# Gate products of a product-key expert layer: the layout of the one-hots and of the numbers and gates they are made from

## The chip, the cores and the metric

The kernel runs on one core of one Trainium2 chip, as one launch. The metric is the time of that launch on the device in microseconds (us); the median of the runs is what counts. TensorE multiplies matrices into PSUM (the accumulation memory), VectorE, ScalarE and GpSimd do elementwise work, and SyncE issues the DMAs. In the views of the profile these are PE (matmuls), PEld (the weight loads of TensorE), DVE, ACT, POOL and SP.

## The reference, cut to what matters

The reference is a transformer block with an attention, a state space mixer and a layer of product-key experts, then two more blocks. The change touches the experts alone:

```python
def peer_mixer(xn, w_query, sub_keys, u_tab, v_tab):
    ...                                  # t = 256 tokens, d = 1024
    vals, idx = lax.top_k(s, PEER_TOPK)  # per head: 16 best of 128 keys on each side
    ...
    i1 = jnp.take_along_axis(idx[:, :, 0], pos // PEER_TOPK, axis=-1)
    i2 = jnp.take_along_axis(idx[:, :, 1], pos % PEER_TOPK, axis=-1)
    expert = (i1 * N_SUB_KEYS + i2).reshape(t, PEER_HEADS * PEER_TOPK)
    gate = jax.nn.softmax(best, axis=-1).reshape(t, PEER_HEADS * PEER_TOPK)
    ...
        a = jnp.einsum('cd,ced->ce', xb, u_tab[eb]).astype(jnp.float32)
        w = (gb * jax.nn.gelu(a, approximate=False)).astype(xb.dtype)
        return jnp.einsum('ce,ced->cd', w, v_tab[eb])
```

Each token has 8 heads x 16 choices = 128 choices, each with a first number i1 and a second number i2 (0 to 127) and a gate. There are 128 x 128 experts.

## The kernel before, in words

The kernel gathers no rows. It computes the activation of every expert for every token, multiplies it by a gate that is zero for experts that were not chosen, and multiplies the result by the whole second table. The function `peer` holds both passes. The tile `store` has, for each partition (the first number), 128 x 256 values: second number by token.

First pass (`gemm_t(128, 8, xh, xl, evict, step=step)`): 128 steps, one for each second number. Each step takes one 512 KB piece of the first table, which SyncE loads, ScalarE rounds to a high part `whi` (L121, two halves) and VectorE or GpSimd subtracts to a low part `wlo` (L123); three buffers of each exist. TensorE then does 24 matmuls of a 128 x 128 weight with 256 tokens (L206 to L208), `evict` applies the GELU on ScalarE (L979, L982), and, for tokens whose gates are known already, VectorE multiplies by the gate (L980). After each step `step` runs pieces of the background work: first `topk`, which finds the choices in two halves of 128 tokens, chiefly on VectorE, and then the gate products, spread evenly over the steps up to number 126.

`topk` ends each half with three TensorE transposes (L1096) of i1, i2 and the gates into PSUM, with the choice on the partition and the token along the row. L1097 copies both kinds of numbers to the 16-bit tile `ids`, L1098 and L1099 write the gate, times 1024, as a high and a low 16-bit part to `gts`.

A gate product is made by `quad(q)` for four tokens at a time, 64 times. For one token the 128 x 128 gates are the product of two one-hots over the choices: A (choice by first number), which is the weight that TensorE loads, and B (choice by second number, each row times the choice's gate, as a high part Bh and a low part Bl), which TensorE moves through. So a quad has 8 matmuls of 128 x 128 with 128 columns (L964, L965), each with a weight load of its own, into one PSUM tile `g`. VectorE multiplies what the first pass has already stored by it (L969) and ScalarE copies the rest (L971). `onehots(q)` makes the operands on VectorE one quad ahead, in two instructions of 1024 elements on each partition: L951 compares `io4` (the numbers 0 to 127, each four times) with the numbers of four tokens, for A and for the unscaled B at once; L952 multiplies by both gate parts. In these tiles the four tokens are innermost: for one token both A and B are read with a step of four 16-bit elements.

```python
v.tensor_tensor(out=AB, in0=io4.unsqueeze(1).to_broadcast(both), in1=b(ids), op=OP.is_equal)
v.tensor_tensor(out=B, in0=AB[:, 1].unsqueeze(1).to_broadcast(both), in1=b(gts), op=OP.mult)
```

Second pass: 128 steps of `gemm_acc` with the second table (L274 to L276, 512 columns each), whose weights come from `store` (L1009, L1010). It begins when all gates are in `store`. Layers of the other block follow.

The order of instructions on each engine is set by the planner of the tile framework, from the order in the program and from priorities (background work has a later one, `LATE`); engines work through their lists in order and wait for each other by semaphores.

Of the kernel before, what the change touches and what calls it, by code (L numbers as in the profile page):

```python
# [9 lines left out]
F16 = mybir.dt.float16  # L10
U32 = mybir.dt.uint32
AF = mybir.ActivationFunctionType
OP = mybir.AluOpType
# [4 lines left out]
T = 256  # L18
# [50 lines left out]
XR = 4  # L69
# [129 lines left out]
class Kernel:  # L199
# [698 lines left out]
    def peer(self):  # L898
        tc, nc, a = self.tc, self.nc, self.a
        v, g, s, te = nc.vector, nc.gpsimd, nc.scalar, nc.tensor  # L900
        self.bg = Background(tc, LATE)
        with ExitStack() as outer:
            pst = outer.enter_context(tc.tile_pool(name="pstore", bufs=1))
            store = pst.tile([128, 128, T], F32, name="store")
            self.tail_base = 76
            flat = store[:, self.tail_base:].rearrange("p a b -> p (a b)")
            off = [0]

            def scratch(shape, dt=F32):
                n = int(np.prod(shape[1:]))  # L910
                x = flat[:, off[0]:off[0] + n]
                off[0] += n
                if dt != F32:
                    x = x.bitcast(dt)
                if len(shape) == 2:
                    return x
                names = "abcd"[:len(shape) - 1]
                kw = {c: d for c, d in zip(names, shape[1:])}
                return x.rearrange(f"p ({' '.join(names)}) -> p {' '.join(names)}", **kw)

            with ExitStack() as ctx:
                w = ctx.enter_context(tc.tile_pool(name="pu", bufs=1))
                self.acc, tp, gp = self.banks(0, 1, 2), self.banks(7, 6), self.banks(3, 4, 5)
                xh, xl = self.tokens()
                for i in range(2):
                    self.norm_h(i, self.gain, xh, xl, tp)
                iota = scratch([128, 128])
                nc.sync.dma_start(iota, a["iota"])
                sk = scratch([128, 8, 128])
                nc.sync.dma_start(sk, a["subkeys"])  # L930
                io4 = w.tile([128, 128, 4], F16, name="io4")
                v.tensor_copy(io4, iota.unsqueeze(2).to_broadcast([128, 128, 4]))

                qT = scratch([128, 8, T])
                self.gemm_t(8, 8, xh, xl, lambda m, ps: s.copy(qT[:, m], ps))

                ids = w.tile([128, 2, T], F16, name="ids")
                gts = w.tile([128, 2, T], F16, name="gts")
                self.bg.add(self.topk(w, tp, scratch, qT, sk, iota, ids, gts))
                done = {"t": 0, "c": 0, "q": 0, "oh": {}, "from": None}  # L940

                spare = self.const.tile([128, 2, 2, 128, 4], F16, name="spare", tag="gain")
                both = [128, 2, 128, 4]

                def onehots(q):


                    b = lambda x: x[:, :, 4 * q:4 * q + 4].unsqueeze(2).to_broadcast(both)
                    AB = self.stay.tile(both, F16, name="oh", tag="xr", bufs=XR)
                    B = spare[:, q % 2]  # L950
                    v.tensor_tensor(out=AB, in0=io4.unsqueeze(1).to_broadcast(both), in1=b(ids), op=OP.is_equal)  # L951
                    v.tensor_tensor(out=B, in0=AB[:, 1].unsqueeze(1).to_broadcast(both), in1=b(gts), op=OP.mult)  # L952
                    done["oh"][q] = AB[:, 0], B[:, 0], B[:, 1]

                def quad(q):
                    c = done["c"]
                    if q not in done["oh"]:
                        onehots(q)
                    if q + 1 < T // 4:
                        onehots(q + 1)  # L960
                    A, Bh, Bl = done["oh"].pop(q)
                    ps = gp.tile([128, 4, 128], F32, name="g", tag="g")
                    for t in range(4):
                        te.matmul(ps[:, t], A[:, :, t], Bh[:, :, t], start=True, stop=False)  # L964
                        te.matmul(ps[:, t], A[:, :, t], Bl[:, :, t], start=False, stop=True)  # L965
                    p = ps.rearrange("p t i -> p i t")
                    o = store[:, :, 4 * q:4 * q + 4]
                    if c:
                        v.scalar_tensor_tensor(o[:, :c], p[:, :c], 1.0 / 1024, o[:, :c], op0=OP.mult, op1=OP.mult)  # L969
                    if c < 128:  # L970
                        s.activation(o[:, c:], p[:, c:], AF.Copy, scale=1.0 / 1024)  # L971
                    done["t"] = 4 * q + 4
                    done["q"] = q + 1

                def evict(m, ps):
                    t = done["t"]
                    if t:
                        tmp = w.tile([128, T], F32, name="gt", tag="gt", bufs=2)
                        s.activation(tmp[:, :t], ps[:, :t], AF.Gelu)  # L979
                        v.tensor_tensor(out=store[:, m, :t], in0=tmp[:, :t], in1=store[:, m, :t], op=OP.mult)  # L980
                    if t < T:
                        s.activation(store[:, m, t:], ps[:, t:], AF.Gelu)  # L982
                    done["c"] = m + 1

                def step():
                    c = done["c"]
                    self.bg.step(STEP(c))
                    if done["from"] is None:
                        if not self.bg.q:
                            done["from"] = c  # L990
                        return
                    want = (T // 4 * (c - done["from"])) // (LAST - done["from"])
                    while done["q"] < min(want, T // 4):
                        quad(done["q"])

                self.gemm_t(128, 8, xh, xl, evict, step=step)
                while done["q"] < T // 4:
                    quad(done["q"])

            with ExitStack() as ctx:  # L1000
                w = ctx.enter_context(tc.tile_pool(name="pv", bufs=1))
                ps = self.acc4(5, 6, 7, 3)
                self.next_gain("attn_norm_0")
                parts = {}

                def split(c):
                    wh = w.tile([128, T], F32R, name="wh", tag="wh", bufs=3)
                    wl = w.tile([128, T], F32R, name="wl", tag="wl", bufs=3)
                    s.copy(wh, store[:, c])  # L1009
                    v.tensor_tensor(out=wl, in0=store[:, c], in1=wh.bitcast(F32), op=OP.subtract)  # L1010
                    parts[c] = wh, wl

                def lhs(c):
                    if c == 0:
                        split(0)
                        split(1)
                    if c + 2 < 128:
                        split(c + 2)
                    return parts[c]

                self.gemm_acc(range(128), Once(lhs), ps, self.residual)

    def topk(self, w, tp, scratch, qT, sk, iota, ids, gts):
        nc = self.nc
        v, g, s, te = nc.vector, nc.gpsimd, nc.scalar, nc.tensor
# [23 lines left out]
        for i in range(2):  # L1049
            ts = slice(128 * i, 128 * i + 128)  # L1050
            for hg in range(2):
                ps = [tp.tile([128, 4, 128], F32, name="tp", tag="tp") for _ in range(2)]
# [8 lines left out]
            for h in range(8):  # L1061
                for k in range(2):
# [4 lines left out]
                                in0=vals[:, h, 0].unsqueeze(2).to_broadcast([128, 16, 16]),  # L1067
                                in1=vals[:, h, 1].unsqueeze(1).to_broadcast([128, 16, 16]), op=OP.add)
# [3 lines left out]
            p = pos.rearrange("p h k -> p (h k)")  # L1072
# [5 lines left out]
            for k in range(2):  # L1078
                v.tensor_tensor(out=eq, in0=pf[:, k].unsqueeze(1).to_broadcast([128, 16, 16, 8]),
                                in1=io16.unsqueeze(2).to_broadcast([128, 16, 16, 8]), op=OP.is_equal)  # L1080
# [13 lines left out]
            ps = tp.tile([128, 4, 128], F32, name="tp", tag="tp")  # L1094
            for k in range(3):
                te.transpose(ps[:, k], e3[:, k], self.ident)  # L1096
            v.tensor_copy(ids[:, :, ts], ps[:, 0:2])  # L1097
            v.tensor_scalar(gts[:, 0, ts], ps[:, 2], 1024.0, None, op0=OP.mult)  # L1098
            v.scalar_tensor_tensor(gts[:, 1, ts], ps[:, 2], 1024.0, gts[:, 0, ts], op0=OP.mult, op1=OP.subtract)  # L1099
            yield  # L1100


# [569 lines left out]
```

## Time and profile before

| what | us |
|---|---|
| median of 3 runs | 1787.24 (1787.05 to 1788.32) |
| the profiled execution | 1782.35 |
| its span, first to last instruction | 1780.6 |
| PE busy | 1703.5 (96%) |
| PEld busy | 1488.6 (84%) |
| DVE busy | 1086.8 (61%) |
| ACT busy | 869.0 (49%) |
| POOL busy | 638.6 (36%) |

The times of rows come from the profiled execution. In a group of instructions the first number is the busy time, the second the mean of one, and after the bar stands the engine's idle time just before them and what ended it. A matmul's recorded duration is longer than its share of the stream, since matmuls overlap: the distance between starts tells what one costs. The first gate product starts 478.0 us after the start of the span and the last at 765.9 us.

### The profile page before, as it was taken

To read this page: it belongs to the slowest core of one execution; us is meant where nothing else is said; L and a number is where in the kernel's file an instruction comes from. 1 tells how busy PE (TensorE), PEld (TensorE's weight loads), DVE (VectorE), ACT (ScalarE), POOL (GpSimd) and SP (SyncE) were. 2 spreads that over 40 slices of the span, in tenths; PEclk is the share of its full clock that TensorE was granted. 3 is DMA by queue.
4 is the path that set the end of the run, shared out by engine and by line. 5 is a ranking of instruction groups with operands and counts; after the bars stand their busy time and mean duration, and the time that the engine had idled before them with its cause. 6 is when DMAs were issued, how large, how long until landed. Compare 5 with 4: busy or idle time off the path is not lost.

```text
span 1780.6 us, 29967 instructions
## 1 busy us (share of the span) xinstructions
PE 1703.5 (96%) x10732; PEld 1488.6 (84%) x10732; DVE 1086.8 (61%) x2496; ACT 869.0 (49%) x2048; POOL 638.6 (36%) x529
## 2 busy tenths in 40 slices
PE   7989998989899999999999999899999999999998
PEld 4457987988899999988888888787899878779986
DVE  6877443589777778855555555677754246875422
ACT  2113544544454444445555555556565455656643
POOL 1020375677400000034444444331444443145443
PEclk9989999999999999999999999999999999999999
DMA  7322445444544444456665656534456664335554
GB/s 228 109 80 72 142 133 166 154 156 143 156 150 144 143 145 149 146 166 190 195 195 192 196 192 192 177 96 143 150 182 190 189 194 139 119 119 190 189 190 142
DMA packets 81537, 282.33 MB, mean 159 GB/s; under 512 B 9659, under 2 KB 12524, under 8 KB 81388
## 3 DMA queue, kind: packets, MB, share of 16 engines
q1 hardware_dynamic: 81388, 280.41, 49.5%
q8 instruction: 85, 1.39, 0.3%
q14 instruction: 64, 0.52, 0.1%
HBM read 279.30 MB, written 1.07 MB: 157 GB/s over the span
## 4 chain that ended last, share of the span: by engine, by line
PE 77%; DVE 12%; POOL 4%; issue 3%; ACT 2%; DMA 2%; POOLq 0%; SPq 0%; DVEq 0%; ACTq 0%
PE acc L276 10%; PE acc L275 10%; PE acc L274 10%; PE acc L208 10%; PE acc L206 10%; PE acc L207 10%; PE acc L219 2%; POOL wlo L123 2%; PE g L964 2%; PE g L965 2%; PE o L1390 1%; PE acc L242 1%; PE acc L243 1%; PE acc L244 1%; DVE wlo L123 1%
## 5 line engine op out<-in xcount | busy, mean ns | idle before, releaser
L123 POOL TENSOR_TENSOR wlo<-raw,whi 128x512 fp32r<-128x512 f32 (+2 forms) x420 | 554.2, 1333 | 913.2 <-ACT whi L121 884.3
L121 ACT CAST whi<-raw 128x512 fp32r<-128x512 f32 (+2 forms) x940 | 544.7, 613 | 436.6 <-PE acc L207 179.3
L123 DVE TENSOR_TENSOR wlo<-raw,whi 128x512 fp32r<-128x512 f32 (+1 forms) x520 | 407.4, 797 | 326.8 <-ACT whi L121 316.0
L208 PE MATMUL acc<-xh,wlo 128*128 128x256 f32 x1664 | 473.7, 285 | 12.5 <-POOL wlo L123 7.3
L206 PE MATMUL acc<-xh,whi 128*128 128x256 f32 x1664 | 478.2, 288 | 2.6 <-ACT whi L121 1.9
L207 PE MATMUL acc<-xl,whi 128*128 128x256 f32 x1664 | 472.3, 284 | 0.1
L208 PEld LDWEIGHTS acc<-xh,wlo 128*128 128x128 f32 x1664 | 320.7, 193 | 15.3 <-POOL wlo L123 8.7
L206 PEld LDWEIGHTS acc<-xh,whi 128*128 128x128 f32 x1664 | 321.5, 194 | 4.3 <-ACT whi L121 2.4
L207 PEld LDWEIGHTS acc<-xl,whi 128*128 128x128 f32 x1664 | 321.2, 193 | 0.6 <-DVE xl L325 0.3
L274 PE MATMUL acc<-whi,wh 128*128 128x512 f32 x512 | 199.8, 390 | 2.7 <-ACT wh L1009 2.7
L275 PE MATMUL acc<-wlo,wh 128*128 128x512 f32 x512 | 199.9, 390 | 0.0
L276 PE MATMUL acc<-whi,wl 128*128 128x512 f32 x512 | 199.9, 391 | 0.0
L1009 ACT CAST wh<-store 128x256 fp32r<-128x256 f32 x128 | 51.9, 407 | 161.3 <-PE acc L275 160.4
L1010 DVE TENSOR_TENSOR wl<-store,wh 128x256 fp32r<-128x256 f32 x128 | 54.2, 425 | 115.6 <-ACT wh L1009 115.5
L274 PEld LDWEIGHTS acc<-whi,wh 128*128 128x128 f32 x512 | 96.5, 188 | 22.9 <-ACT wh L1009 2.9
L276 PEld LDWEIGHTS acc<-whi,wl 128*128 128x128 f32 x512 | 96.6, 189 | 20.0
L275 PEld LDWEIGHTS acc<-wlo,wh 128*128 128x128 f32 x512 | 96.4, 188 | 20.2
L275 PE MATMUL acc<-wlo,fh 128*128 128x512 f32 x256 | 99.7, 390 | 0.0
L276 PE MATMUL acc<-whi,fl 128*128 128x512 f32 x256 | 99.7, 389 | 0.0
L274 PE MATMUL acc<-whi,fh 128*128 128x512 f32 x256 | 99.6, 389 | 0.0
L219 PE MATMUL acc<-xt,raw 128*128 128x256 f32 x320 | 76.2, 386 | 0.0
L219 PEld LDWEIGHTS acc<-xt,raw 128*128 128x128 f32 x320 | 58.8, 191 | 12.0 <-issue 3.9
(377 smaller groups left out, 2508.2 us busy)
## 6 DMA issues: line engine op xcount, KB each, us to landing
raw<-in_peer_u_dram SPq DMA_DIRECT2D x128, 512.0 KB, 3.6
raw<-in_peer_v_dram SPq DMA_DIRECT2D x128, 512.0 KB, 3.6
raw<-in_w_ff_dram SPq DMA_DIRECT2D x128, 512.0 KB, 3.9
raw<-in_w_out_dram SPq DMA_DIRECT2D x24, 512.0 KB, 4.0
raw<-in_w_in_g_dram SPq DMA_DIRECT2D x16, 512.0 KB, 3.6
raw<-in_w_in_qkv_dram SPq DMA_DIRECT2D x12, 512.0 KB, 3.6
raw<-in_w_attn_branch_dram SPq DMA_DIRECT2D x8, 512.0 KB, 3.6
raw<-in_peer_w_query_dram SPq DMA_DIRECT2D x8, 512.0 KB, 4.0
```

Of the source, the lines that this page charges most:

```text
L121: nc.scalar.copy(hi[:, x], src[:, x])
L123: eng.tensor_tensor(out=lo[:, x], in0=src[:, x], in1=hi[:, x].bitcast(F32), op=OP.subtract)
L206: t.matmul(ps, wh, xh, start=first, stop=False)
L207: t.matmul(ps, wh, xl, start=False, stop=False)
L208: t.matmul(ps, wl, xh, start=False, stop=last)
L219: self.nc.tensor.matmul(ps, wh[:, k, m], xh[:, k], start=k == 0, stop=k == kt - 1)
L274: t.matmul(ps[i][n], xh[:, ts], w[0][:, ns], start=first, stop=False)
L275: t.matmul(ps[i][n], xh[:, ts], w[1][:, ns], start=False, stop=False)
L276: t.matmul(ps[i][n], xl[:, ts], w[0][:, ns], start=False, stop=last)
L964: te.matmul(ps[:, t], A[:, :, t], Bh[:, :, t], start=True, stop=False)
L1009: s.copy(wh, store[:, c])
L1010: v.tensor_tensor(out=wl, in0=store[:, c], in1=wh.bitcast(F32), op=OP.subtract)
```

## The change

B gets another layout: for each group of four neighbouring second numbers a run for token 0, then for tokens 1, 2 and 3, each run with the four numbers side by side. A keeps its layout. The unscaled B is now made apart from A, by a comparison of `ion` (numbers 0 to 127 in that order, every group of four repeated for four tokens) with i2 kept four times for each token, so that the 16 values of four tokens lie side by side. The gates are kept fourfold too. `onehots` has three VectorE instructions, of 512, 1024 and 512 elements on each partition. Bh and Bl are handed to the matmuls as 32 groups of 4 elements, 16 elements from group to group. The end of `topk` has four VectorE instructions in place of three, and three of them write 512 elements. The new tiles take 5.6 KB more on each partition, and the program is built with a dynamic DMA scratch of 1024.

```diff
+                ion = w.tile([128, 32, 4, 4], F16, name="ion")
+                v.tensor_copy(ion, iota.rearrange("p (a i) -> p a i", i=4).unsqueeze(2).to_broadcast([128, 32, 4, 4]))
+                ion = ion.rearrange("p a t i -> p a (t i)")
...
-                ids = w.tile([128, 2, T], F16, name="ids")
-                gts = w.tile([128, 2, T], F16, name="gts")
+                ids = w.tile([128, T], F16, name="ids"), w.tile([128, T, 4], F16, name="ids4")
+                gts = w.tile([128, 2, T, 4], F16, name="gts")
...
-                spare = self.const.tile([128, 2, 2, 128, 4], F16, name="spare", tag="gain")
-                both = [128, 2, 128, 4]
+                spare = self.const.tile([128, 2, 2, 32, 16], F16, name="spare", tag="gain")
+                four = lambda x, q: x[..., 4 * q:4 * q + 4, :].rearrange(
+                    "p k t i -> p k (t i)" if len(x.shape) == 4 else "p t i -> p (t i)")
...
-                    b = lambda x: x[:, :, 4 * q:4 * q + 4].unsqueeze(2).to_broadcast(both)
-                    AB = self.stay.tile(both, F16, name="oh", tag="xr", bufs=XR)
+                    AB = self.stay.tile([128, 2, 512], F16, name="oh", tag="xr", bufs=XR)
+                    A, E = AB[:, 0].rearrange("p (n t) -> p n t", t=4), AB[:, 1].rearrange("p (a x) -> p a x", x=16)
                     B = spare[:, q % 2]
-                    v.tensor_tensor(out=AB, in0=io4.unsqueeze(1).to_broadcast(both), in1=b(ids), op=OP.is_equal)
-                    v.tensor_tensor(out=B, in0=AB[:, 1].unsqueeze(1).to_broadcast(both), in1=b(gts), op=OP.mult)
-                    done["oh"][q] = AB[:, 0], B[:, 0], B[:, 1]
+                    v.tensor_tensor(out=E, in0=ion, in1=four(ids[1], q).unsqueeze(1).to_broadcast([128, 32, 16]),
+                                    op=OP.is_equal)
+                    v.tensor_tensor(out=B, in0=E.unsqueeze(1).to_broadcast([128, 2, 32, 16]),
+                                    in1=four(gts, q).unsqueeze(2).to_broadcast([128, 2, 32, 16]), op=OP.mult)
+                    v.tensor_tensor(out=A, in0=io4, in1=ids[0][:, 4 * q:4 * q + 4].unsqueeze(1).to_broadcast([128, 128, 4]),
+                                    op=OP.is_equal)
+                    done["oh"][q] = A, *[B[:, n].rearrange("p a (t i) -> p a t i", i=4) for n in range(2)]
...
-                        te.matmul(ps[:, t], A[:, :, t], Bh[:, :, t], start=True, stop=False)
-                        te.matmul(ps[:, t], A[:, :, t], Bl[:, :, t], start=False, stop=True)
+                        te.matmul(ps[:, t].rearrange("p (a i) -> p a i", i=4), A[:, :, t], Bh[:, :, t], start=True, stop=False)
+                        te.matmul(ps[:, t].rearrange("p (a i) -> p a i", i=4), A[:, :, t], Bl[:, :, t], start=False, stop=True)
...
-            v.tensor_copy(ids[:, :, ts], ps[:, 0:2])
-            v.tensor_scalar(gts[:, 0, ts], ps[:, 2], 1024.0, None, op0=OP.mult)
-            v.scalar_tensor_tensor(gts[:, 1, ts], ps[:, 2], 1024.0, gts[:, 0, ts], op0=OP.mult, op1=OP.subtract)
+            four = lambda x: x.unsqueeze(2).to_broadcast([128, 128, 4])
+            v.tensor_copy(ids[0][:, ts], ps[:, 0])
+            v.tensor_copy(ids[1][:, ts], four(ps[:, 1]))
+            v.tensor_scalar(gts[:, 0, ts], four(ps[:, 2]), 1024.0, None, op0=OP.mult)
+            v.scalar_tensor_tensor(gts[:, 1, ts], four(ps[:, 2]), 1024.0, gts[:, 0, ts], op0=OP.mult, op1=OP.subtract)
...
-    nc = bacc.Bacc("TRN2", target_bir_lowering=False, num_devices=1)
+    nc = bacc.Bacc("TRN2", target_bir_lowering=False, num_devices=1, dynamic_dma_scratch_size=1024)
```

## Rows read from the trace of the kernel before

**Rows 1.** The page: busy us of each engine, share of the span, instructions.
```profile
PE 1703.5 (96%) x10732; PEld 1488.6 (84%) x10732; DVE 1086.8 (61%) x2496; ACT 869.0 (49%) x2048; POOL 638.6 (36%) x529
```
**Rows 2.** The page: chain of waits that ended last, share of the span by line.
```profile
PE acc L276 10%; PE acc L275 10%; PE acc L274 10%; PE acc L208 10%; PE acc L206 10%; PE acc L207 10%; PE acc L219 2%; POOL wlo L123 2%; PE g L964 2%; PE g L965 2%; PE o L1390 1%; PE acc L242 1%; PE acc L243 1%; PE acc L244 1%; DVE wlo L123 1%
```
**Rows 3.** Windows: stretch, length; PE, PEld, DVE, ACT, POOL busy; clock; DMA share, GB/s.
```profile
478.00:768.00 290.00, 290.00 (x2430) 286.82 (x2429) 221.13 (x426) 137.23 (x382) 1.29 (x1) 1.00 0.47 147
```
**Rows 4.** Instruction groups of PE, 478 to 768 us: busy, mean ns, idle before.
```profile
L206 PE MATMUL acc<-xh,whi 128*128 128x256 f32 x638 | 185.7, 291 | 0.0
...
L965 PE MATMUL g<-spare,oh 128*128 128x128 f16 x256 | 64.6, 298 | 0.0
```
**Rows 5.** Timeline of one quad: start us, duration us, engine, line, operation.
```profile
601.67 0.11 PEld L964 LDWEIGHTS <-oh 128*128 128x128 f16 x1
601.68 0.29 PE L964 MATMUL g<-spare,oh 128*128 128x128 f16 x1
601.69 0.13 PEld L965 LDWEIGHTS <-oh 128*128 128x128 f16 x1
601.78 0.30 PE L965 MATMUL g<-spare,oh 128*128 128x128 f16 x1
601.79 0.12 PEld L964 LDWEIGHTS <-oh 128*128 128x128 f16 x1
...
602.50 0.30 PE L965 MATMUL g<-spare,oh 128*128 128x128 f16 x1
602.50 0.21 PEld L206 LDWEIGHTS acc<-xh,whi 128*128 128x128 f32 x1
602.54 0.37 PE L206 MATMUL acc<-xh,whi 128*128 128x256 f32 x1
602.63 0.20 PEld L207 LDWEIGHTS acc<-xl,whi 128*128 128x128 f32 x1
602.75 0.28 PE L207 MATMUL acc<-xl,whi 128*128 128x256 f32 x1
602.87 0.28 PE L208 MATMUL acc<-xh,wlo 128*128 128x256 f32 x1
```
**Rows 6.** Timeline of PE in the second pass, 512 columns.
```profile
849.18 0.39 PE L274 MATMUL acc<-whi,wh 128*128 128x512 f32 x1
...
850.54 0.39 PE L274 MATMUL acc<-whi,wh 128*128 128x512 f32 x1
```
**Rows 7.** Timeline, matmuls of 32 columns and their weight loads, six merged.
```profile
1228.04 0.75 PEld L1323 LDWEIGHTS acc<-kc,qT 128*128 128x128 f32 x6
...
1228.09 0.81 PE L1323 MATMUL acc<-kc,qT 128*128 128x32 f32 x6
```
**Rows 8.** Instruction groups of DVE: first three from 478 to 768 us.
```profile
L123 DVE TENSOR_TENSOR wlo<-raw,whi 128x512 fp32r<-128x512 f32 x158 | 108.6, 687 | 67.6 <-ACT whi L121 67.3
L952 DVE TENSOR_TENSOR spare<-oh,gts 128x1024 f16<-128x1024 f16 x62 | 42.3, 683 | 0.0
L951 DVE TENSOR_TENSOR oh<-io,ids 128x1024 f16<-128x1024 f16 x60 | 41.0, 683 | 0.0
...
L1010 DVE TENSOR_TENSOR wl<-store,wh 128x256 fp32r<-128x256 f32 x128 | 54.2, 425 | 115.6 <-ACT wh L1009 115.5
...
L1379 DVE COPY P<-tp 128x512 f32<-128x512 f32 x24 | 16.3, 684 | 4.3 <-PE tp L1378 4.2
...
L1097 DVE CAST ids<-tp 128x256 f16<-128x256 f32 x2 | 0.8, 420 | 4.1 <-PE tp L1096 4.1
...
L1098 DVE TENSOR_SCALAR gts<-tp 128x128 f16<-128x128 f32 x2 | 0.6, 280 | 0.0
```
**Rows 9.** Waits of PE, 290 to 480 us: total us, times, longest.
```profile
PE acc L208 <- POOL wlo L123: 7.3, 7, 1.6
PE acc L208 <- DVE wlo L123: 5.2, 2, 3.3
```

## The prediction

> **What bounds the kernel now.** I read the page first. PE is busy for 96% of the span and no other engine for more than 61% [rows 1]; by lines, the chain of waits spends its time in the streams of the two passes, and the gate products L964 and L965 have 2% each [rows 2]. Then the windows: the gate products all lie between 478 and 768 us, and there PE is busy for the whole 290.00 us at the full granted clock (1.00, the 2.4 GHz level), with DVE at 221.13, ACT at 137.23, POOL at 1.29 and the DMA engines at 0.47 [rows 3]. The groups of PE in that stretch show no idle time before them [rows 4]. So here a matmul that takes less of the stream shortens the kernel by that much, until another engine is full, and work added on DVE costs nothing while its results come in time.
>
> What one gate product costs is read from starts, not durations. In the timeline of a quad the eight start at 601.68 to 602.50: seven intervals in 0.82 us, 117 ns each. The matmuls of the pass, 256 columns in the rounded 32-bit type, start 120 ns apart (602.75 to 602.87) [rows 5]. Those of 512 columns in the second pass start 227 ns apart (six intervals, 849.18 to 850.54) [rows 6]. The difference, 107 ns for 256 columns, is 0.418 ns a column, one clock at 2.4 GHz; what is left, 13 ns, comes with each matmul. A gate product has 128 columns: one clock each would be 53.5 + 13 = 66.5 ns. It takes 117, that is (117 - 13) / 128 = 0.81 ns a column, two clocks.
>
> The weight load could be the cause instead, so I look at a stream that waits for its loads. Before matmuls of 32 columns six loads take 0.75 us together [rows 7]; one load alone is 0.19, as for L206 [rows 5], which leaves five intervals of 112 ns. That is near 117. In the quad each load starts with the matmul before it (601.78 and 601.79) and lasts 0.12, so a chain of loads would look like this too. But the second matmul starts at 601.78, before its own load ends (601.69 + 0.13 = 601.82), and the first two loads end at 601.78 and 601.82, 40 ns apart at this rounding [rows 5]: a 16-bit load can follow another far sooner than in 117 ns. I take it that the moved operand, read with a step of four elements, sets the 117 ns.
>
> The Trainium skill (Advanced Engine Details and Errata, Memory Cachelines) states that SBUF has lines of 16 bytes and that two hits in a line suffice for full speed. The old layout has a step of 8 bytes, so two hits in each line, and by that rule it is read at full speed already and the new layout can give nothing; the trace shows 117 ns where full speed would be 66.5, and I follow the trace, but the rule is the first rival below.
>
> **The change part by part.**
>
> The matmuls. B is now read in runs of four neighbours, with 16 elements from run to run; A, the weights, keeps its step. No row shows such a read. One end is one clock a column, 66.5 ns; without the 13 ns, 53.5. The other end is today's 117; that it is worse is a rival. I take 66.5, since rows 6 show this rate wherever neighbours lie together, and each run is of neighbours. Which intervals shrink: the seven inside a quad. The step from the last product to the first matmul of the pass does not, because that one's load starts with the last product (602.50) and its own matmul begins its work 0.13 us later, when the next load starts (602.63) [rows 5]. So 64 x 7 = 448 intervals by 117 - 66.5 = 50.5 ns: -22.6 us. With 53.5 ns it is 448 x 63.5 = -28.4.
>
> The Trainium skill (TensorE: Matmul & The Clock Gate, Back-to-back issue gap) gives about 81 ns for a sustained pair of load and matmul with 128 columns. By that figure, as an estimate, the sum would be 448 x 36 = -16 us; no run here shows it.
>
> The one-hots. Two DVE instructions of 1024 16-bit elements at 0.683 us become three, of 512, 1024 and 512 [rows 8]. 1024 such elements take what 512 32-bit elements take (0.687, L123), so two a clock; 512 then cost what 256 32-bit ones do, 0.425 (L1010). The inner run that repeats is 16 instead of 4, step one in both, and I expect no other rate. 64 x (0.425 + 0.683 + 0.425 - 2 x 0.683) = 64 x 0.167 = +10.7 us on DVE, nearly all in the stretch: 221.1 + 10.7 = 232 of the 267 us that are left, 87%. Beside PE it costs nothing: `onehots` runs one quad ahead, and PE waits for none of it today. Behind these instructions on DVE wait the halves of `wlo`, and behind them L208; three buffers stand between, and DVE itself is idle for 67.3 us waiting for ACT's `whi` [rows 8]. If that cover is gone, a rival below has the price.
>
> The end of `topk`. L1097 to L1099 take 0.42 + 0.28 + 0.28 us [rows 8] (L1099 as L1098). After: one copy of 128 elements (0.28) and three that read 128 values of PSUM four times and write 512, for which a copy of 512 from PSUM, 0.684 (L1379), is the nearest row [rows 8]: 2.33, so +1.35 us for each half of the tokens. The second half falls into the full stretch and is covered. After the first, up to 480 us, DVE works through `topk`, and PE waits there for `wlo`, 5.2 us of it for DVE's [rows 9]. The delay is 1.35 plus three one-hots made early (3 x 0.167), 1.85 us: all of it on the path, or none. I take half, +0.9. The single copy for `ion` (no more than the 0.684) comes at the beginning of the pass, before `topk`, and I take it as hidden; on the path it would be 0.7.
>
> The room. The tiles grow by 5.6 KB a partition, and the dynamic DMA scratch shrinks. The weights come through the queue that SyncE issues; nothing in the pass issues DMAs from POOL. I cost it at 0, with -1 to +2 for another placement and another order of the planner.
>
> The sum against the profiled execution (1782.35, its span 1780.6 and 1.75 around it): -22.6 + 0.9 = -21.7, so 1760.6. The median of the runs is 4.9 above that execution: 1787.2 - 21.7 = 1765.5.
>
> **The rivals.**
>
> Nothing is gained, because the weight load or a step common to all sets 117 ns. For it: 112 ns between loads of 128 columns, the step of A is kept, the 120 ns of the pass are near. The Trainium skill's rule on lines, above, speaks for it too. Against it: the first two 16-bit loads end 40 ns apart, and a matmul starts before its load's end. Then 1787.2 + 0 to 1.9, about 1788.
>
> DVE becomes the bound, and the kernel gets slower. The place is the stretch of the quads: if the 67.3 us that DVE waits for ACT are part of a loop and not spare, the stretch is 221.1 + 10.7 + 67.3 = 299 us in place of 290: 1796. It decides once `wlo` arrives later than three buffers allow, some 5 us late. For it: DVE at 87%. Against it: ACT waits for PE's release of `whi`, so these waits shrink with PE, and PE shows no wait there now [rows 4]. In a mild form it eats a third to two thirds of the gain: 1773 to 1780.
>
> The new read is slower. If each of the 32 runs costs over 104 / 32 = 3.25 ns (four columns at one clock are 1.67), the matmul is slower than now; at 5 ns a run it is 173 ns and the sum 448 x 56 = +25, 1812. Nothing in the trace speaks for it; the old read jumps at every element and costs two clocks.
>
> **How the numbers follow.** Forecast (intervals of 53 to 81 ns) 0.70, with 1758 to 1773 as its own range; mild form 0.08; nothing gained 0.13; DVE bound 0.05; slower read 0.04. A measurement of this kernel tells 0.2% (3.6 us) from no change. Faster is 0.70 + 0.08 = 0.78, same 0.13, slower 0.09. The range goes from 1757 to 1788: it leaves out the two slower cases, about half of "nothing gained" and a little at the lower end.
>
> **What would show it.** Right: starts inside a quad 60 to 80 ns apart, 478 to 768 shorter by 16 to 28 us and still full of PE, DVE at about 87% of it with 64 groups of 0.42, 0.68 and 0.42 us, no PE wait on `wlo` or on the one-hots there. The step from L965 to L206 and L207 as before. Wrong: starts still 117 ns apart (the loads); starts short but PE idle before L208 or L964 (DVE); starts longer than 117 (the runs); or a different time outside the first pass (the planner's order).

## The result and the profile after

The changed kernel takes 1763.81 us (1763.10 to 1764.02, 4 runs) against 1787.78 us of the kernel before (1787.05 to 1788.87, 4 runs): a ratio of 0.9861, 95% interval 0.9847 to 0.9875, 24.0 us off the medians. The forecast was 1765.5. Run twice more beside other kernels it took 1761.81 and 1762.84.

From the page, the busy time of each engine (as in [rows 1]) and the chain of waits by line (as in [rows 2]). The gate products (now L973 and L974) are gone from the lines of 1% and more.

```profile
PE 1682.0 (95%) x10732; PEld 1465.1 (83%) x10732; DVE 1094.2 (62%) x2563; ACT 868.3 (49%) x2048; POOL 638.4 (36%) x529
...
PE acc L206 10%; PE acc L276 10%; PE acc L274 10%; PE acc L275 10%; PE acc L208 10%; PE acc L207 10%; PE acc L219 3%; POOL wlo L123 2%; PE acc L243 1%; PE acc L244 1%; PE acc L242 1%; DVE wlo L123 1%; ACT whi L121 1%; DMA raw<-in_w_out_dram 1%; PE o L1401 1%
```

The windows of the stretch with the gate products, columns as in [rows 3]:

```profile
483.00:746.00 263.00, 263.00 (x2412) 260.25 (x2411) 224.61 (x485) 135.84 (x379) 0.00 (x0) 1.00 0.52 159
```

PE still fills it and is the bound; DVE has 85% (76% before). The timeline of one quad, to set beside [rows 5]:

```profile
603.15 0.25 PE L973 MATMUL g<-spare,oh 128*128 128x128 f16 x1
...
603.24 0.23 PE L974 MATMUL g<-spare,oh 128*128 128x128 f16 x1
...
603.30 0.22 PE L973 MATMUL g<-spare,oh 128*128 128x128 f16 x1
...
603.60 0.22 PE L974 MATMUL g<-spare,oh 128*128 128x128 f16 x1
603.60 0.19 PEld L206 LDWEIGHTS acc<-xh,whi 128*128 128x128 f32 x1
603.63 0.36 PE L206 MATMUL acc<-xh,whi 128*128 128x256 f32 x1
603.71 0.19 PEld L207 LDWEIGHTS acc<-xl,whi 128*128 128x128 f32 x1
603.83 0.28 PE L207 MATMUL acc<-xl,whi 128*128 128x256 f32 x1
```

The first interval is 90 ns, the six others 60 (603.24 to 603.60). Before, in [rows 5], the first was 100 and the six others 120 (601.78 to 602.50), 117 on the average. From the last product to L207 it is 0.23 us (0.25 before). So a quad has 0.45 + 0.23 = 0.68 us in place of 0.82 + 0.25 = 1.07, and 64 x 0.39 = 25.0 us.

The new VectorE groups, 483 to 746 us, to set beside [rows 8]:

```profile
L123 DVE TENSOR_TENSOR wlo<-raw,whi 128x512 fp32r<-128x512 f32 x158 | 108.7, 688 | 38.0 <-ACT whi L121 36.9
L958 DVE TENSOR_TENSOR spare<-oh,gts 128x1024 f16<-128x1024 f16 x62 | 42.4, 685 | 0.0
L956 DVE TENSOR_TENSOR oh<-ion,ids 128x512 f16<-128x512 f16 x60 | 25.1, 419 | 0.0
L960 DVE TENSOR_TENSOR oh<-io,ids 128x512 f16<-128x512 f16 x60 | 25.1, 419 | 0.0
```

The copies of the choices at the end of `topk`, by their groups from 300 to 490 us:

```profile
L1109 DVE TENSOR_SCALAR gts<-tp 128x512 f16<-128x512 f32 x1 | 0.7, 682 | 0.0
L1108 DVE CAST ids<-tp 128x512 f16<-128x512 f32 x1 | 0.7, 681 | 0.0
...
L1107 DVE CAST ids<-tp 128x128 f16<-128x128 f32 x1 | 0.3, 292 | 4.3 <-PE tp L1105 4.3
```

What DVE waits for ACT fell from 67.3 us to 36.9. The waits of PE from 290 to 480 us, to set beside [rows 9]:

```profile
PE acc L208 <- POOL wlo L123: 6.3, 5, 1.9
PE acc L208 <- DVE wlo L123: 5.6, 2, 3.9
```

The two profiled executions differ by less than the medians: 1782.35 to 1763.95, 18.4 us. The first quad begins at 483.2 us, 5.2 later than before, and 2.7 of that is there before the pass begins: `io4` is copied at 283.1 us in one and 285.8 in the other. The windows from 14 to 18 us, of before and then of after, show where it starts, in code that the change does not touch:

```profile
14.00:18.00 4.00, 4.00 (x17) 2.83 (x17) 3.97 (x12) 0.59 (x1) 1.50 (x1) 1.00 0.56 143
```

```profile
14.00:18.00 4.00, 4.00 (x9) 2.28 (x9) 3.96 (x12) 0.59 (x1) 1.50 (x1) 1.00 0.56 138
```

Nine matmuls run there in place of 17. From 290 to 296 us the granted clock differs as well, 0.93 and 0.50 (the 1.2 GHz level), again before and after:

```profile
290.00:296.00 6.00, 6.00 (x49) 6.00 (x49) 0.59 (x1) 1.80 (x4) 2.45 (x2) 0.93 0.00 0
```

```profile
290.00:296.00 6.00, 5.71 (x26) 5.71 (x27) 2.42 (x6) 0.82 (x2) 0.00 (x0) 0.50 0.30 87
```

Of the eleven traces of the new layout one has the quick start (that with VectorE's comparison doubled, below), and the three without it all have. So the new layout does not force the slow start; whether it makes it likelier stays open. The length of the quads, which the start does not touch, is compared from here on: first to last start 287.9 us before (478.0 to 765.9) and 262.9 after (483.2 to 746.1). Behind the last start it is 1.3 us longer after, so the spans, 1780.6 and 1762.1, differ by 25.0 - 5.2 - 1.3 = 18.5.

### The profile page after: what moved, and what is told of

Read it like the earlier page. It is cut to its first block, busy times and chain, and to the rows that moved or that the text cites. A ratio compares the mean times of both kernels' runs of the same rounds, so it can differ in the third digit from the quotient of the medians.

```text
span 1762.1 us, 30035 instructions
## 1 busy us (share of the span) xinstructions
PE 1682.0 (95%) x10732; PEld 1465.1 (83%) x10732; DVE 1094.2 (62%) x2563; ACT 868.3 (49%) x2048; POOL 638.4 (36%) x529
## 3 DMA queue, kind: packets, MB, share of 16 engines
HBM read 279.30 MB, written 1.07 MB: 159 GB/s over the span
## 4 chain that ended last, share of the span: by engine, by line
PE 76%; DVE 12%; POOL 4%; issue 3%; DMA 3%; ACT 2%; SPq 0%; POOLq 0%; DVEq 0%; ACTq 0%
PE acc L206 10%; PE acc L276 10%; PE acc L274 10%; PE acc L275 10%; PE acc L208 10%; PE acc L207 10%; PE acc L219 3%; POOL wlo L123 2%; PE acc L243 1%; PE acc L244 1%; PE acc L242 1%; DVE wlo L123 1%; ACT whi L121 1%; DMA raw<-in_w_out_dram 1%; PE o L1401 1%
## 5 line engine op out<-in xcount | busy, mean ns | idle before, releaser
L207 PE MATMUL acc<-xl,whi 128*128 128x256 f32 x1664 | 473.7, 285 | 0.1
L208 PEld LDWEIGHTS acc<-xh,wlo 128*128 128x128 f32 x1664 | 322.1, 194 | 14.4 <-POOL wlo L123 7.6
L207 PEld LDWEIGHTS acc<-xl,whi 128*128 128x128 f32 x1664 | 322.4, 194 | 0.6 <-DVE xl L325 0.3
```

Source lines behind the costliest of these rows:

```text
L207: t.matmul(ps, wh, xl, start=False, stop=False)
L208: t.matmul(ps, wl, xh, start=False, stop=last)
```

## The experiments

**The old read with all the new VectorE work.** The matmuls read the new tile with the old step of four.

```diff
-                    done["oh"][q] = A, *[B[:, n].rearrange("p a (t i) -> p a t i", i=4) for n in range(2)]
+                    done["oh"][q] = A, *[B[:, n].rearrange("p a x -> p (a x)").rearrange("p (j t) -> p j t", t=4) for n in range(2)]
```

> All of the changed kernel's VectorE work, but the moved one-hots are read with a step of four elements from the same tile (the gate values are then wrong). Theory 1, the step of the moved read sets what a product costs: the starts go back to about 117 ns, six of seven intervals in a quad grow by 58 and the first by about 18, 64 x 0.366 = +23.4 us, so about 1787 us, and what it lies above the kernel before is what the added VectorE work costs (I take 0 to 1.9). Theory 2, the gain comes from elsewhere (the one-hots made apart, the planner's order, the room): about 1764.

It took 1788.52 us; against the kernel before on that chip (1787.01) 1.0008, 0.9999 to 1.0017. The whole gain is gone with the read alone, and the VectorE work added costs between -0.2 and 3.0 us. Eight starts in its timeline span 0.82 us again, 117 ns for each interval on the average:

```profile
602.47 0.29 PE L973 MATMUL g<-spare,oh 128*128 128x128 f16 x1
...
603.29 0.30 PE L974 MATMUL g<-spare,oh 128*128 128x128 f16 x1
```

The changed kernel beside it:

> The changed kernel once more, beside the three that vary it. Both theories: about 1763.8 us, starts inside a quad about 60 ns apart (the first interval about 89).

1761.81 us, 0.9856 (0.9838 to 0.9873).

**The room alone.** The kernel before with `dynamic_dma_scratch_size=1024`.

> The kernel before with the smaller dynamic DMA scratch alone. Both theories: 1787 us within 2 us, starts 117 to 119 ns apart. If the room or where tiles lie gave part of the gain, it is below 1784. It also shows again when the kernel before starts its first quad (478.0 us in the first trace of before, 480.1 to 483.6 in all traces of the changed layout): about 478 if the added VectorE work delays it, about 482 if that trace was a quick one.

1787.94 us, 1.0002 (0.9992 to 1.0012): the room gives nothing beyond that interval, -1.4 to 2.1 us. The group of L964 in its trace runs from the same place to the same place as before:

```profile
L964 PE MATMUL g<-spare,oh x256: 285/298/303, 477.9 to 765.8; 128*128 128x128 f16 x128
```

**Which step costs what.** Four kernels change the moved read alone, each by the line shown above and the pattern in the two matmuls.

```text
pairs:     B[:, n] as "p (a t i) -> p a t i", t=4, i=2
step two:  B[:, n] as "p (h j t) -> p h j t", h=2, t=2, read at [:, t // 2, :, t % 2]
step 8:    both parts as "p (j n t) -> p n j t", n=2, t=4
together:  B[:, n] as "p (t j) -> p j t", t=4
```

> The changed kernel with the moved one-hots read in runs of two elements, eight elements from run to run (values wrong). What is fetched at a time decides. If groups of 8 bytes: two elements of each group, full rate, starts 60 ns, 1764 us. If lines of 16 bytes: two elements a line, as with the old step of four, so starts 117 ns, 1787 us. If words of 4 bytes: both halves used, 60 ns.

1787.05 us, 0.9996 (0.9986 to 1.0006), -2.5 to 1.1 us. Its quads are as long as before, so this is a second bound on what the added VectorE work costs. Seven intervals in 0.83 us, 119 ns:

```profile
601.91 0.29 PE L973 MATMUL g<-spare,oh 128*128 128x128 f16 x1
...
602.74 0.30 PE L974 MATMUL g<-spare,oh 128*128 128x128 f16 x1
```

> The changed kernel with the moved one-hots read with a step of two elements (values wrong). Groups of 8 bytes: two of each group, 60 ns, 1764 us. Lines of 16 bytes: four of each, 60 ns. Words of 4 bytes, or neighbours needed: one of each word, 117 ns, 1787 us.

1760.86 us, 0.9853 (0.9837 to 0.9869). Six intervals behind the first in 0.36 us, 60 ns, with no two neighbours read after each other:

```profile
602.11 0.22 PE L974 MATMUL g<-spare,oh 128*128 128x128 f16 x1
...
602.47 0.22 PE L974 MATMUL g<-spare,oh 128*128 128x128 f16 x1
```

> The changed kernel with the moved one-hots read with a step of eight elements, over the tile of both gate parts (values wrong). Groups of 8 bytes or words of 4: one element of each, two clocks a column as with a step of four, starts about 117 ns, 1787 us. Lines of 16 bytes: one of each line in place of two, four clocks a column, starts about 220 ns, about 1830 us.

1847.07 us, 1.0334 (1.0317 to 1.0351), 17 us above the highest time expected. Seven intervals in 1.61 us, 230 ns where 220 were expected; and the step from the last product to L207 grew too, to 0.36 us from 0.25. The two make 64 x (0.79 + 0.11) = 57.6 us:

```profile
604.75 0.40 PE L973 MATMUL g<-spare,oh 128*128 128x128 f16 x1
...
606.36 0.41 PE L974 MATMUL g<-spare,oh 128*128 128x128 f16 x1
...
606.72 0.28 PE L207 MATMUL acc<-xl,whi 128*128 128x256 f32 x1
```

> The changed kernel with the moved one-hots of a token read as 128 elements side by side (values wrong). Theory 1, a run of four costs nothing over this: starts 60 ns, 1763.8 us within 2 us. Rival, each of the 32 runs costs something: starts 56 ns or less, 2 us or more off.

1761.57 us, 0.9850 (0.9833 to 0.9866); six intervals behind the first in 0.34 us, 57 ns (56 over all its quads), where the runs of four have 60:

```profile
607.14 0.22 PE L974 MATMUL g<-spare,oh 128*128 128x128 f16 x1
...
607.48 0.22 PE L974 MATMUL g<-spare,oh 128*128 128x128 f16 x1
```

Its quads last 261.2 us against 262.9, by the group of its products:

```profile
L973 PE MATMUL g<-spare,oh x256: 218/219/248, 481.6 to 742.8; 128*128 128x128 f16 x128
```

So the rival is right in a small part: the 32 runs cost 4 ns a product over reading all together, which the times, by 448, cannot tell. Pairs and step two decide between the groups: both use two elements of each 8 bytes that they touch, and one is slow and the other fast. So neither groups of 8 bytes nor neighbours count, but lines of 16 bytes, counted from the tile's start:

| moved read of 128 elements | lines | elements of each | interval, ns |
|---|---|---|---|
| step of eight | 128 | 1 | 230 |
| step of four (before); pairs | 64 | 2 | 117; 119 |
| step of two; fours (after) | 32 | 4 | 60; 60 |
| together | 16 | 8 | 57 |

The 117 is no difference to pairs: over all the quads of their traces both reads have 107 ns for the first interval and 119 for the others. From 64 lines to 128 a further line costs (230 - 119) / 64 = 1.73 ns, and from 32 to 64 it is (119 - 60) / 32 = 1.84. Thirty-two lines at 1.73 are 55 ns, about the 53.5 of the 128 columns, and there the product takes 60. Lines of 32 bytes do not fit: pairs and fours touch 32 of these each, spread over the same 1 KB, and differ by a factor of two.

**The weights.** A read as 128 elements side by side.

```diff
-                    done["oh"][q] = A, *[
+                    done["oh"][q] = AB[:, 0].rearrange("p (t n) -> p n t", t=4), *[
```

> The changed kernel with the weights of a gate product read as 128 elements side by side (the values are then wrong). Theory 1, the moved read sets the interval: starts stay at 60 ns and the time at 1763.8 within 2 us. Rival, after the change the weight load with its step of four is the bound: starts fall under 57 ns, 448 x 4 = 2 us or more off.

1761.44 us, 0.9852 (0.9834 to 0.9870). The starts fall to 57 ns, and the first interval to 70: 262.9 us of quads become 261.0 (483.0 to 744.0). The step of the weights costs 2 us in all beside this moved read, so the rival has a small part of the truth, but only now that the moved read is quick. It is no floor of the load's own: with the moved read together and the weights still at a step of four, the starts behind the first are as close.

```profile
602.04 0.23 PE L973 MATMUL g<-spare,oh 128*128 128x128 f16 x1
602.11 0.22 PE L974 MATMUL g<-spare,oh 128*128 128x128 f16 x1
...
602.45 0.22 PE L974 MATMUL g<-spare,oh 128*128 128x128 f16 x1
```

**More work on VectorE.** The comparison for E, the unscaled one-hot, is issued twice, and in another kernel four times.

```diff
                     v.tensor_tensor(out=E, in0=ion, in1=four(ids[1], q).unsqueeze(1).to_broadcast([128, 32, 16]),
                                     op=OP.is_equal)
+                    v.tensor_tensor(out=E, in0=ion, in1=four(ids[1], q).unsqueeze(1).to_broadcast([128, 32, 16]),
+                                    op=OP.is_equal)
```

> The changed kernel with the comparison for the unscaled one-hot done twice: 64 more VectorE instructions of 0.42 us, 27 us, so 254 of the 268 us of the stretch. Theory 1, VectorE's waits for ScalarE's whi are spare there: within 3 us of 1763.8, PE still shows next to no wait from 483 to 746 us. Rival, they are part of a loop: VectorE is the bound and the time goes up by most of the 27 us, to 1780 or more.

1764.11 us, 0.9873 (0.9856 to 0.9891), 2.3 above the changed kernel on that chip, with intervals that overlap. The windows of its stretch: DVE at 240.72 of 260 (93%), PE full; its quads last 262.9 us like those of the changed kernel (480.1 to 743.0).

```profile
483.00:743.00 260.00, 260.00 (x2384) 257.29 (x2383) 240.72 (x541) 134.48 (x376) 0.00 (x0) 1.00 0.52 159
```

Its `wlo` group in the same stretch has 16.4 us of waits for ACT left:

```profile
L123 DVE TENSOR_TENSOR wlo<-raw,whi 128x512 fp32r<-128x512 f32 x156 | 105.9, 687 | 18.1 <-ACT whi L121 16.4
```

> The changed kernel with the comparison for the unscaled one-hot done four times: 3 x 64 more VectorE instructions; one more took the busy time from 228 to 248 us in a stretch of 270, so three more need about 290. VectorE is then full, and the stretch must grow by about 20 us or more: 1782 us or above. It puts a price on the rival that VectorE is the bound; if the time stays under 1770, VectorE has more room than its busy time tells.

1783.24 us, 0.9967 (0.9955 to 0.9979). Here VectorE is the bound: in the windows of its quads, 279.73 of 281 us busy, with PE at 272.72.

```profile
491.00:772.00 281.00, 272.72 (x2452) 266.24 (x2452) 279.73 (x666) 139.29 (x385) 4.22 (x2) 1.00 0.49 150
```

The waits of PE in the same stretch show whom it waits for (sum in us, count, longest):

```profile
PE acc L208 <- DVE wlo L123: 8.1, 13, 1.4
```

So VectorE's waits for `whi` are spare: the work of the doubled comparison went into them and the quads kept their length. With four comparisons VectorE has 1.3 us idle in the stretch, and PE waits. Where between the two it begins to cost time was not measured.

**Tokens in pairs.** What the table suggests as a kernel that computes all: two tokens side by side, so that A and B are both read with a step of two and nothing is kept fourfold. Built on the kernel before.

```diff
-                    v.tensor_tensor(out=AB, in0=io4.unsqueeze(1).to_broadcast(both), in1=b(ids), op=OP.is_equal)
-                    v.tensor_tensor(out=B, in0=AB[:, 1].unsqueeze(1).to_broadcast(both), in1=b(gts), op=OP.mult)
+                    v.tensor_tensor(out=AB, in0=io2.unsqueeze(1).to_broadcast(both), op=OP.is_equal,
+                                    in1=ids[:, q].rearrange("p k (h t) -> p (k h) t", t=2).unsqueeze(2).to_broadcast(both))
+                    v.tensor_tensor(out=B, in0=AB[:, 2:4].unsqueeze(1).to_broadcast([128, 2, 2, 128, 2]), op=OP.mult,
+                                    in1=gts[:, q].rearrange("p n (h t) -> p n h t", t=2).unsqueeze(3)
+                                    .to_broadcast([128, 2, 2, 128, 2]))
...
-                        te.matmul(ps[:, t], A[:, :, t], Bh[:, :, t], start=True, stop=False)
+                        te.matmul(ps[:, t], A[:, t // 2, :, t % 2], Bh[:, t // 2, :, t % 2], start=True, stop=False)
```

> A kernel that follows from the runs on steps: two tokens are kept side by side in place of four, so weights and moved one-hots are both read with a step of two elements, four of them in each line of 16 bytes. Neither numbers nor gates are kept fourfold, there are two VectorE instructions of 1024 elements for a quad as before the change, and the scratch is left as it was. Theory, the lines touched set the cost: starts 57 to 60 ns, 64 x 0.17 = 11 us less VectorE work than the changed kernel, 1757 to 1762 us. If runs of neighbours were needed: 117 ns and 1787.

> The changed kernel again, to compare the kernel with tokens in pairs with on one chip: 1762 to 1764 us.

1759.74 us, 0.9844 (0.9826 to 0.9862), and the changed kernel beside it 1762.84, 0.9858 (0.9837 to 0.9878). The intervals overlap, so the times do not show it faster; the trace does for the quads, 261.4 us against 262.9, by the group of its products:

```profile
L966 PE MATMUL g<-spare,oh x256: 218/220/232, 478.1 to 739.5; 128*128 128x128 f16 x128
```

The windows of its stretch have DVE at 218.37 of 260 us:

```profile
483.00:743.00 260.00, 260.00 (x2393) 257.33 (x2392) 218.37 (x422) 134.94 (x378) 1.30 (x1) 1.00 0.52 161
```

## Why the prediction was right

**The cause.** The moved read set the 117 ns. It was inferred from the first two weight loads of a quad and from a matmul that began before its load's end; the old read put back alone brings back 26.7 us (1788.52 against 1761.81). The first rival, that the loads set the interval, falls: the weights are read in the same way in both.

**Why the read was slow** was wrong in the prediction. It said two clocks a column, and took from this that neighbours are needed. What counts is the lines touched: pairs of neighbours are as slow as the old step, and a step of two without neighbours is as fast as runs of four. The change gave the gain since four elements share a line. That it has runs of four is in this sense luck: by the prediction's reason a layout in pairs would have had the same forecast, and it measured 1787.05. The Trainium skill (Advanced Engine Details and Errata, Memory Cachelines) names this line of 16 bytes; but where it asks for at least two hits in a line, which the prediction took as enough, the runs show 117 and 119 ns with two and 60 with four. The measurement decides: for this read two are not enough and four are; three was not run.

**The matmuls' term.** -22.6 us was forecast, 448 intervals from 117 to 66.5 ns. Measured are the seven together from 0.82 us to 0.45, which makes 64 x 0.37 = 23.7, and 0.02 us less on the way from the last product to L207, which I had taken as unchanged: 1.3 more, 25.0 together. The 66.5 was too high because of the 13 ns that I took over from the 32-bit matmuls; with the moved operand side by side the products show 56 or 57, about 3 ns over the columns. The Trainium skill's 81 ns for a pair of load and matmul of 128 columns (TensorE: Matmul & The Clock Gate, Back-to-back issue gap), which stands at the upper end of the forecast's intervals, is not what this stream shows, 60. The profiled execution was forecast at 1760.6 and took 1763.95, with the slow start; the medians differ by 24.0 where 21.7 was forecast.

**The one-hots.** 0.425, 0.683 and 0.425 us forecast, 0.419, 0.685 and 0.419 measured, covered as said. DVE came to 85% (87% forecast).

**The end of `topk`.** 0.28 + 3 x 0.684 forecast; 0.29 and 0.68 each measured. The waits of PE from 290 to 480 us sum to 15.3 us after (the two rows shown and 3.4 of smaller ones, for ACT) and 14.4 before (those of [rows 9] and 1.9). That equals the +0.9 taken, but half of a delay was a guess, and the stretch also begins at another clock. The times bound all of this only to between -0.2 and 3.0 us (the old read) and -2.5 and 1.1 (pairs).

**The room** was taken as nothing and shows nothing.

**The rivals.** VectorE as the bound: no, and the run with four comparisons shows its price, a stretch of 281 us for a busy time of 280. Runs that cost more than a column each: no, 4 ns a product over reading all together. What no run here settles is why the start of the kernel, before the pass, is quick in four traces (`io4`, or `io2` of the kernel with pairs, copied at 282.8 to 283.1 us) and slow in ten (284.4 to 287.1); it stands beside a count of matmuls that halves while the recorded clock is 1.00.

## What to carry to other kernels

Before you accept the cost of a small matmul, subtract its columns at the rate of a dense stream in the same trace; what is left over may be the pattern by which the moved operand is read. Count the 16-byte lines that a read of 128 columns touches: with at least four 16-bit elements used of each, neighbours or every second one, the read was within 4 ns of full rate here, and each line beyond that cost 1.7 to 1.8 ns. Choose the interleave that the producer needs for its own speed as small as that allows; two tokens side by side would have done, without the fourfold copies.

## What the runs showed of the hardware that was not expected

The moved read of 16-bit elements pays by lines of 16 bytes, 1.7 to 1.8 ns each beyond 32 for 128 columns; elements of a line need not be neighbours. The weight load with the same step of four cost only 3 ns of each interval and 20 ns of the first in a quad, visible once the moved read was quick; with the moved operand side by side the intervals behind the first were 56 or 57 ns in spite of that step. The 13 ns that each rounded 32-bit matmul has over its columns (120 for 256, 227 for 512) are not there for 16-bit ones.
